# K and V of eight heads on 128 partitions: 8 KB rows, V under four quarter masks, one KV product of 260 columns

## Chip, cores, metric

One core of one Trainium2 chip. The metric is device time in microseconds (us). "Span" is the time from the first to the last instruction of a profiled execution. Ratios are the mean time of one kernel's fast runs over that of the other's fast runs of the same rounds, so they are not quite the ratio of the medians quoted beside them.

## The reference

Linear attention with ReLU features, batch 8, 12 heads, sequence 512, head size 64, all fp32:

```python
Q_feat = np.maximum(0, Q); K_feat = np.maximum(0, K)
KV    = np.einsum('bhkd,bhkv->bhdv', K_feat, V)
K_sum = np.sum(K_feat, axis=2)
numerator   = np.einsum('bhqd,bhdv->bhqv', Q_feat, KV)
denominator = np.einsum('bhqd,bhd->bhq', Q_feat, K_sum)
return (numerator / (denominator[:, :, :, None] + 1e-10)).astype(np.float32)
```

Each of Q, K, V and the output is 12.58 MB. The arithmetic is small; the traffic is not.

## The kernel before

It works in 12 octets (eight heads). Q is loaded by octets (a partition holds 32 rows of 64, 8 KB in DRAM), K and V by half octets (16 rows, 4 KB). All loads but the first are cast to bf16 on the way, from GpSimd's queue. To multiply several heads at once, K is written twice under a mask (even and odd heads) and V twice (left and right half of the partitions), with a column of ones that gives the sum of K. The product of a half octet accumulates over 16 rows into 130 columns.

```python
    def load_kv(g):                                   # a half octet
        k_sb[g] = kin.tile([P, R, D], bf16, name="k_sb")
        nc.gpsimd.dma_start(out=k_sb[g].rearrange("p r d -> p (r d)"), in_=Kr[g])
        v_sb[g] = vin.tile([P, R, D], bf16, name="v_sb")
        nc.gpsimd.dma_start(out=v_sb[g].rearrange("p r d -> p (r d)"), in_=Vr[g])
    ...
    def prep(g):
        for s in range(2):
            nc.vector.tensor_scalar(kf[g][:, :, s, :], k_sb[g], scalar1=0.0,
                                    scalar2=mask[:, 0, s:s + 1], op0=Alu.max, op1=Alu.mult)
        nc.vector.tensor_scalar(vo[g % NB][:, :, 0, 0:D], v_sb[g], scalar1=mask[:, 1, 0:1], ...)
    def prep_act(g):
        nc.scalar.activation(vo[g % NB][:, :, 1, 0:D], v_sb[g], Act.Copy, scale=mask[:, 1, 1:2])
    def mm_kv(g):
        ps_kv[g] = pkv.tile([P, 2, D1], fp32, name="ps_kv")
        for r in range(R):
            nc.tensor.matmul(ps_kv[g], kf[g][:, r, :, :]..., vo[g % NB][:, r, :, :], ...)
    def evac_kv(g):                                   # 4 copies, PSUM to SBUF, on ACT
        ...
    def store(o, o_sb):
        if o + DELAY < NO:                            # waits until K of octet o + 5 is there
            nc.sync.dma_start(out=scratch, in_=k_sb[2 * (o + DELAY)][0:1, 0, :])
        ...
    for o in range(NO + 1):
        mm_kv(2 * o); evac_kv(2 * o)
        mm_out(o - 1, 0); norm(o - 1, 0, o_sb)
        prep(2 * o + 2); prep_act(2 * o + 2)
        mm_out(o - 1, 1); norm(o - 1, 1, o_sb)
        mm_kv(2 * o + 1); evac_kv(2 * o + 1)
        for i in range(2):
            transp(o, i); evac_qt(o, i)
        prep(2 * o + 3); prep_act(2 * o + 3)
        mm_out(o - 1, 2); norm(o - 1, 2, o_sb); store(o - 1, o_sb)
```

(The conditions for the first and last rounds of the loop are cut, and some arguments, marked by dots.) The order in this loop is the order on each engine. The stores are held back on purpose: until the loads end, each waits for K five octets ahead, so that some five octets of output are still to be stored when the last load lands.

Of the kernel before, what the change touches and what calls it, by code (L numbers as in the profile page):

```python
# [10 lines left out]
def kernel(  # L11
# [7 lines left out]
    nc = tc.nc  # L19
    B, H, S, D = Q.shape  # L20
    assert D == 64
    P = 128
    D1 = D + 1
    NH = B * H


    R = S * 4 // P
    RQ = S * 8 // P
    NHG = 4
    U = RQ // 2  # L30
    NG = NH // NHG
    NO = NG // 2
    assert NO * 8 == NH and R == 16 and RQ == 32
    DELAY = 5
    F32 = 2

    fp32 = mybir.dt.float32
    bf16 = mybir.dt.bfloat16
    Act = mybir.ActivationFunctionType
    Alu = mybir.AluOpType  # L40

    def pool(name, bufs, **kw):
        return ctx.enter_context(tc.tile_pool(name=name, bufs=bufs, **kw))

    consts = pool("consts", 1)
    qin = pool("qin", 7)
    kin = pool("kin", 12)
    vin = pool("vin", 12)
    kfp = pool("kfp", 4)
    rcp = pool("rcp", 4)  # L50
    outp = pool("outp", DELAY + 2)
    pkv = pool("pkv", 2, space=bass.MemoryType.PSUM)
# [3 lines left out]
    def view(X, f):  # L56
        return X.rearrange("b h s d -> (b h s d)").rearrange("(n p f) -> n p f", p=P, f=f)

    Qr, Kr, Vr, Or = view(Q, RQ * D), view(K, R * D), view(V, R * D), view(out, RQ * D)

    ident = consts.tile([P, P], bf16, name="ident")
    NB = 4
    NK = 4
    NZ = 2




    vo = [consts.tile([P, R, 2, D1], bf16, name=f"vo{i}") for i in range(NB)]
    kvf = [consts.tile([P, NHG * 2 * D1], bf16, name=f"kvd{i}") for i in range(NK)]  # L70
    kvd = [x.rearrange("p (t s c d) -> p t s c d", t=2, s=2, c=2) for x in kvf]
    mask = consts.tile([P, 2, 2], fp32, name="mask")
    scratch = consts.tile([1, D], bf16, name="scratch")


# [4 lines left out]

    q_sb, k_sb, v_sb = {}, {}, {}

    def load_kv(g):
        k_sb[g] = kin.tile([P, R, D], bf16, name="k_sb")
        nc.gpsimd.dma_start(out=k_sb[g].rearrange("p r d -> p (r d)"), in_=Kr[g])  # L85
        v_sb[g] = vin.tile([P, R, D], bf16, name="v_sb")
        nc.gpsimd.dma_start(out=v_sb[g].rearrange("p r d -> p (r d)"), in_=Vr[g])  # L87

    def load_q(o):
        q_sb[o] = qin.tile([P, U, 2 * D], bf16, name="q_sb")  # L90
        nc.gpsimd.dma_start(out=q_sb[o].rearrange("p u f -> p (u f)"), in_=Qr[o])  # L91


    for g in range(F32):
        kv = outp.tile([P, 2, R, D], fp32, name="kv_first", tag="o_sb")
        k_sb[g], v_sb[g] = kv[:, 0], kv[:, 1]
        nc.sync.dma_start(out=k_sb[g].rearrange("p r d -> p (r d)"), in_=Kr[g])
        nc.scalar.dma_start(out=v_sb[g].rearrange("p r d -> p (r d)"), in_=Vr[g])
    load_q(0)
    make_identity(nc, ident)  # L100
    for o in range(1, NO):
        load_kv(2 * o)
        load_kv(2 * o + 1)
        load_q(o)

    def zero(i):
        if i == 0:
            for h in range(NHG):
                for s in range(2):
                    nc.vector.memset(mask[32 * h:32 * h + 32, 0, s:s + 1], 1.0 if h % 2 == s else 0.0)  # L110
            for t in range(2):
                nc.vector.memset(mask[:, 1, t:t + 1], 0.0)
                nc.vector.memset(mask[64 * t:64 * t + 64, 1, t:t + 1], 1.0)
        if i < NB:
            nc.vector.memset(vo[i][:, :, :, D:D1], 0.0)
            for t in range(2):
                nc.vector.memset(vo[i][64 * t:64 * t + 64, :, t, D:D1], 1.0)
        nc.vector.memset(kvf[i].bitcast(fp32), 0.0)  # L118

    def zero_q(i):  # L120
        nc.vector.memset(qtf[i].rearrange("p z f -> p (z f)").bitcast(fp32), 0.0)  # L121

    kf, ps_kv, ps_qt, ps_out = {}, {}, {}, {}

    def prep(g):
        kf[g] = kfp.tile([P, R, 2, D], bf16, name="kf")
        for s in range(2):
            nc.vector.tensor_scalar(kf[g][:, :, s, :], k_sb[g], scalar1=0.0,  # L128
                                    scalar2=mask[:, 0, s:s + 1], op0=Alu.max, op1=Alu.mult)
        nc.vector.tensor_scalar(vo[g % NB][:, :, 0, 0:D], v_sb[g], scalar1=mask[:, 1, 0:1],  # L130
                                scalar2=None, op0=Alu.mult)

    def prep_act(g):
        nc.scalar.activation(vo[g % NB][:, :, 1, 0:D], v_sb[g], Act.Copy, scale=mask[:, 1, 1:2])  # L134

    def mm_kv(g):
        ps_kv[g] = pkv.tile([P, 2, D1], fp32, name="ps_kv")
        for r in range(R):
            nc.tensor.matmul(  # L139
                ps_kv[g], kf[g][:, r, :, :].rearrange("p s d -> p (s d)"), vo[g % NB][:, r, :, :],  # L140
                start=(r == 0), stop=(r == R - 1), skip_group_check=True)

    def evac_kv(g):
        for s in range(2):
            for c in range(2):
                nc.scalar.copy(kvd[g % NK][64 * c:64 * c + 64, :, s, c, :],  # L146
                               ps_kv[g][64 * s:64 * s + 64])


    def transp(o, i):  # L150
        ps_qt[o, i] = pqt.tile([P, U // 2, P], bf16, name="ps_qt")
        for u in range(U // 2):
            nc.tensor.transpose(ps_qt[o, i][:, u, :], q_sb[o][:, i * (U // 2) + u, :], ident)  # L153
# [10 lines left out]
    def mm_out(o, j):  # L164
        po = pou.tile([P, 2, 512], fp32, name="ps_out")
        ps_out[o, j] = po
        u0, nu = ROUNDS[j]
        for v in range(nu):
            u, b, c = u0 + v, v // (nu // 2), v % (nu // 2) * 2 * D1
            for z in range(2):  # L170
                for w in range(4):
                    hs = slice(32 * w, 32 * w + 32)
                    h = 2 * w + z
                    nc.tensor.matmul(  # L174
                        po[hs, b, c:c + 2 * D1],
                        qtf[o % NZ][:, z, u * P + 32 * w:u * P + 32 * w + 32],
                        kvd[(2 * o + h // 4) % NK][:, h % 4 // 2, h % 2, :, :],
                        start=(z == 0), stop=(z == 1), skip_group_check=True)

    def norm(o, j, o_sb):  # L180
        u0, nu = ROUNDS[j]
        pv = ps_out[o, j][:, :, 0:nu * D1].rearrange("p b (r d) -> p b r d", d=D1)
        den = rcp.tile([P, 2, nu], fp32, name="den")
        nc.vector.tensor_scalar(den, pv[:, :, :, D], scalar1=1e-10, scalar2=None, op0=Alu.add)  # L184
        rec = rcp.tile([P, 2, nu], fp32, name="rec")
        nc.vector.reciprocal(rec, den)  # L186
        nc.vector.tensor_tensor(  # L187
            o_sb[:, 2 * u0:2 * (u0 + nu)].rearrange("p (b r) d -> p b r d", b=2),
            pv[:, :, :, 0:D],
            rec.unsqueeze(3).to_broadcast([P, 2, nu, D]), op=Alu.mult)  # L190
# [3 lines left out]

    def store(o, o_sb):
        if o + DELAY < NO:
            nc.sync.dma_start(out=scratch, in_=k_sb[2 * (o + DELAY)][0:1, 0, :])
        parts = 2 if o == NO - 1 else 1
        n = RQ // parts
        for j in range(parts):  # L200
            rs = slice(n * j, n * (j + 1))
            nc.sync.dma_start(out=Or[o].rearrange("p (r d) -> p r d", d=D)[:, rs], in_=o_sb[:, rs])

    zero(0)
    prep(0)
    prep_act(0)
    zero(1)
    prep(1)
    prep_act(1)
    zero_q(0)  # L210
    for k in range(2, NK):
        zero(k)
    zero_q(1)

    for o in range(NO + 1):
        ahead = o + 1 < NO
        if o > 0:
            o_sb = outp.tile([P, RQ, D], fp32, name="o_sb", tag="o_sb")
        if o < NO:
            mm_kv(2 * o)  # L220
            evac_kv(2 * o)
        if o > 0:
            mm_out(o - 1, 0)
            norm(o - 1, 0, o_sb)
        if ahead:
            prep(2 * o + 2)
            prep_act(2 * o + 2)
        if o > 0:
            mm_out(o - 1, 1)
            norm(o - 1, 1, o_sb)  # L230
        if o < NO:
            mm_kv(2 * o + 1)
            evac_kv(2 * o + 1)
            for i in range(2):
                transp(o, i)
                evac_qt(o, i)
        if ahead:
            prep(2 * o + 3)
            prep_act(2 * o + 3)
        if o > 0:  # L240
            mm_out(o - 1, 2)
            norm(o - 1, 2, o_sb)
            store(o - 1, o_sb)
# [28 lines left out]
```

## Time and profile before

| | kernel before |
|---|---|
| time, median of 4 runs | 128.07 us |
| span of the profiled run | 126.2 us |
| HBM read, written | 37.75 MB, 12.58 MB |
| mean granted TensorE clock | 0.905 |
| last Q load, last data packet ended | 111.2 us |
| last output ready, last store landed | 120.0, 125.1 us |

The first four rows are from the results and the page. The last two come from the records of single DMA packets and from the timeline. Read with the DMA slices in the prediction below: the sixteen DMA engines work from start to end; what compute must do is to be ready with the last octets while older stores still go out.

### The profile page before, as it was taken

The page shows a single profiled execution, that of the slowest core. Times are in us where ns is not written, and L with a number is a line of the kernel's source. Part 1 is how long each engine was busy: PE and PEld are TensorE (multiplying, and loading weights), DVE is VectorE, ACT ScalarE, POOL GpSimd, SP SyncE. Part 2 cuts the span into 40 slices and gives each one's busy share as a digit, 9 for nine tenths or more (in the row PEclk, how much of TensorE's full clock was granted, in tenths as well). Part 3 has the DMA queues.
Part 4 walks back from the last instruction along what each step waited for, and adds up shares of the span by engine and source line. Part 5 has one row for each costly group of instructions (what it writes and reads, how often), then busy time and mean ns, then how long its engine had stood idle before and what let it go on. Part 6 is the DMA issues. An engine that isn't in the chain of part 4 may idle for free.

```text
span 126.2 us, 4865 instructions
## 1 busy us (share of the span) xinstructions
PE 77.3 (61%) x2112; PEld 68.3 (54%) x2112; DVE 80.6 (64%) x210; ACT 76.9 (61%) x169; POOL 32.1 (25%) x62
## 2 busy tenths in 40 slices
PE   0032917978397956534997647389964793797200
PEld 0041907967386845434986646178953692696100
DVE  3256785698936959673669787528828628774900
ACT  0165891599198798660799949508917925958000
POOL 6902424325243331241143133033113000000000
PEclk9999999999859999996799999955999679769995
DMA  3999999999999999999999999999999999999992
GB/s 106 374 309 213 214 208 209 217 206 218 205 215 209 208 214 324 257 216 325 256 215 301 280 214 281 301 212 214 347 235 216 316 266 216 352 418 410 416 384 104
DMA packets 10757, 32.81 MB, mean 260 GB/s; under 512 B 1392, under 2 KB 1392, under 8 KB 9328
## 3 DMA queue, kind: packets, MB, share of 16 engines
q0 software_dynamic: 8064, 17.83, 73.9%
q1 hardware_dynamic: 2384, 13.63, 27.1%
q10 hardware_dynamic: 288, 1.05, 2.1%
q8 instruction: 16, 0.26, 0.7%
q14 instruction: 5, 0.04, 0.1%
HBM read 37.75 MB, written 12.58 MB: 399 GB/s over the span
## 4 chain that ended last, share of the span: by engine, by line
DMA 32%; PE 27%; issue 13%; ACT 11%; DVE 10%; ACTq 1%; SPq 0%
DMA v_sb<-in_V_dram 25%; PE ps_out L174 13%; PE ps_kv L139 11%; DMA kv_first<-in_K_dram 7%; ACT kvd L146 5%; ACT qt L159 4%; PE ps_qt L153 3%; DVE o_sb L187 3%; DVE qt L121 3%; ACT vo L134 3%; DVE kf L128 2%; DVE vo L130 1%; DVE rec L186 1%; ACTq L267 0%; DVE kvd L118 0%
## 5 line engine op out<-in xcount | busy, mean ns | idle before, releaser
L139 PE MATMUL ps_kv<-vo,kf 128*128 128x130 bf16 x384 | 32.5, 248 | 21.9 <-ACT vo L134 11.7
L174 PE MATMUL ps_out<-kvd,qt 128*32 128x130 bf16 x1536 | 33.7, 243 | 16.7 <-issue 13.3
L139 PEld LDWEIGHTS <-kf 128*128 128x128 bf16 x384 | 27.8, 112 | 25.3 <-DVE vo L130 16.3
L174 PEld LDWEIGHTS <-qt 128*32 128x32 bf16 x1536 | 27.0, 107 | 21.9 <-issue 15.3
L146 ACT CAST kvd<-ps_kv 64x130 bf16<-64x130 f32 x96 | 25.2, 263 | 16.7 <-PE ps_kv L139 14.8
L134 ACT ACTIVATE vo<-v_sb,mask 128x1024 bf16<-128x1024 bf16 x22 | 26.2, 1190 | 13.9 <-DMA v_sb<-in_V_dram 13.8
L187 DVE TENSOR_TENSOR o_sb<-ps_out,rec 128x768 f32<-128x768 f32 (+1 forms) x36 | 31.3, 868 | 1.4
L159 ACT ACTIVATE qt<-ps_qt 128x512 bf16<-128x512 bf16 x48 | 24.8, 603 | 0.3
L128 DVE TENSOR_SCALAR kf<-k_sb,mask 128x1024 bf16<-128x1024 bf16 x44 | 19.1, 476 | 8.6 <-DMA k_sb<-in_K_dram 8.6
L85 POOL DMA_DIRECT2D k_sb<-in_K_dram x22 | 12.8, 583 | 39.1 <-DMA q_sb<-in_Q_dram 24.1
L184 DVE TENSOR_SCALAR den<-ps_out 128x12 f32<-128x12 f32 (+1 forms) x36 | 5.9, 164 | 17.9 <-PE ps_out L174 17.8
L153 PE MATMUL ps_qt<-ident,q_sb 128*128 128x128 bf16 x192 | 15.7, 245 | 2.4 <-issue 2.4
L87 POOL DMA_DIRECT2D v_sb<-in_V_dram x22 | 12.3, 557 | 17.1 <-DMA k_sb<-in_K_dram 7.3
L153 PEld LDWEIGHTS <-q_sb 128*128 128x128 bf16 x192 | 14.0, 112 | 2.6 <-issue 2.5
L130 DVE TENSOR_SCALAR vo<-v_sb,mask 128x1024 bf16<-128x1024 bf16 x22 | 10.6, 481 | 2.1 <-DMA v_sb<-in_V_dram 2.1
L186 DVE RECIPROCAL rec<-den 128x12 f32<-128x12 f32 (+1 forms) x36 | 7.9, 220 | 1.2
L91 POOL DMA_DIRECT2D q_sb<-in_Q_dram x12 | 6.5, 542 | 7.8 <-DMA v_sb<-in_V_dram 4.1
L128 DVE TENSOR_SCALAR kf<-kv_first,mask 128x1024 bf16<-128x1024 f32 x4 | 2.8, 750 | 4.9 <-DMA kv_first<-in_K_dram 4.9
L134 ACT ACT_TABLE_LOAD x1 | 1.3, 1283 | 5.8 <-DMA kv_first<-in_V_dram 5.8
L121 DVE MEMSET qt<- 128x2048 f32 x2 | 3.5, 1765 | 0.8 <-issue 0.8
L134 ACT ACTIVATE vo<-kv_first,mask 128x1024 bf16<-128x1024 f32 x2 | 2.4, 1180 | 2.6 <-DMA kv_first<-in_V_dram 2.6
L130 DVE TENSOR_SCALAR vo<-kv_first,mask 128x1024 bf16<-128x1024 f32 x2 | 1.5, 747 | 0.0
(12 smaller groups left out, 3.5 us busy)
## 6 DMA issues: line engine op xcount, KB each, us to landing
out_dram<-o_sb SPq DMA_DIRECT2D x11, 1024.0 KB, 9.2
q_sb<-in_Q_dram POOLq DMA_DIRECT2D x12, 512.0 KB, 14.9
k_sb<-in_K_dram POOLq DMA_DIRECT2D x22, 256.0 KB, 13.8
v_sb<-in_V_dram POOLq DMA_DIRECT2D x22, 256.0 KB, 13.2
kv_first<-in_V_dram ACTq DMA_DIRECT2D x2, 512.0 KB, 7.3
kv_first<-in_K_dram SPq DMA_DIRECT2D x2, 512.0 KB, 7.0
out_dram<-o_sb SPq DMA_DIRECT2D x2, 512.0 KB, 5.1
scratch<-k_sb SPq DMA_DIRECT2D x7, 0.1 KB, 5.1
```

Of the source, the lines that this page charges most:

```text
L85: nc.gpsimd.dma_start(out=k_sb[g].rearrange("p r d -> p (r d)"), in_=Kr[g])
L87: nc.gpsimd.dma_start(out=v_sb[g].rearrange("p r d -> p (r d)"), in_=Vr[g])
L128: nc.vector.tensor_scalar(kf[g][:, :, s, :], k_sb[g], scalar1=0.0, scalar2=mask[:, 0, s:s + 1], op0=Alu.max, op1=Alu.mult)
L130: nc.vector.tensor_scalar(vo[g % NB][:, :, 0, 0:D], v_sb[g], scalar1=mask[:, 1, 0:1], scalar2=None, op0=Alu.mult)
L134: nc.scalar.activation(vo[g % NB][:, :, 1, 0:D], v_sb[g], Act.Copy, scale=mask[:, 1, 1:2])
L139: nc.tensor.matmul(ps_kv[g], kf[g][:, r, :, :].rearrange("p s d -> p (s d)"), vo[g % NB][:, r, :, :], start=(r == 0), stop=(r == R - 1), s ...
L146: nc.scalar.copy(kvd[g % NK][64 * c:64 * c + 64, :, s, c, :], ps_kv[g][64 * s:64 * s + 64])
L153: nc.tensor.transpose(ps_qt[o, i][:, u, :], q_sb[o][:, i * (U // 2) + u, :], ident)
L159: nc.scalar.activation(qtz[o % NZ][:, z, us, :, z, :], pv[:, :, :, z, :], Act.Relu)
L174: nc.tensor.matmul(po[hs, b, c:c + 2 * D1], qtf[o % NZ][:, z, u * P + 32 * w:u * P + 32 * w + 32], kvd[(2 * o + h // 4) % NK][:, h % 4 // ...
L186: nc.vector.reciprocal(rec, den)
L187: nc.vector.tensor_tensor(o_sb[:, 2 * u0:2 * (u0 + nu)].rearrange("p (b r) d -> p b r d", b=2), pv[:, :, :, 0:D], rec.unsqueeze(3).to_broa ...
```

## The change

Intent: K and V get the 8 KB rows that Q already has (half as many transfers, fewer packets), and the KV product of an octet becomes one accumulation with 260 columns, so that half as many evacuations are needed. The price: a partition now holds one of eight heads, so V must be written four times, each under the mask of a quarter of the partitions. There are fewer buffers too: three half octets of masked K and of V where there were four. Core of the diff:

```diff
-    def load_kv(g):
-        k_sb[g] = kin.tile([P, R, D], bf16, name="k_sb")
-        nc.gpsimd.dma_start(out=k_sb[g]..., in_=Kr[g])
+    def load_kv(o):
+        k_sb[o] = kin.tile([P, RQ, D], bf16, name="k_sb")
+        nc.gpsimd.dma_start(out=k_sb[o]..., in_=Kr[o])
 ... (V alike; the first octet, fp32:)
+    for i in range(2):
+        rs = slice(i * R, (i + 1) * R)
+        nc.sync.dma_start(out=k_sb[0][:, rs], in_=Kr[0].rearrange("p (r d) -> p r d", d=D)[:, rs])
+        nc.scalar.dma_start(out=v_sb[0][:, rs], in_=Vr[0].rearrange("p (r d) -> p r d", d=D)[:, rs])
+    nc.gpsimd.memset(mask_h, 1.0)                     # and two affine_selects on it
     load_q(0)
 ...
-        nc.vector.tensor_scalar(vo[g % NB][:, :, 0, 0:D], v_sb[g], scalar1=mask[:, 1, 0:1], ...)
+        for t in range(NT - 1 - g % 2):               # 3 of 4 quarters, or 2
+            nc.vector.tensor_scalar(vo[g % NB][:, :, t, 0:D], half(v_sb, g),
+                                    scalar1=mask_t[:, t:t + 1], scalar2=None, op0=Alu.mult)
     def prep_act(g):
-        nc.scalar.activation(vo[g % NB][:, :, 1, 0:D], v_sb[g], Act.Copy, scale=mask[:, 1, 1:2])
+        for t in range(NT - 1 - g % 2, NT):           # 1 of 4, or 2
+            nc.scalar.activation(vo[g % NB][:, :, t, 0:D], half(v_sb, g), Act.Copy,
+                                 scale=mask_t[:, t:t + 1])
     def mm_kv(g):
-        ps_kv[g] = pkv.tile([P, 2, D1], fp32, name="ps_kv")
+        if i == 0:
+            ps_kv[o] = pkv.tile([P, NT, D1], fp32, name="ps_kv")
 ... (one evac_kv for an octet, after mm_kv(2 * o + 1))
```

`half(x, g)` is the first or second 16 rows of an octet's tile. Both halves of an octet now come with one transfer of K and one of V.

More of the change, by code (lines that the diff above doesn't have):

```diff
@@ L24 @@
     NH = B * H
-    R = S * 4 // P
     RQ = S * 8 // P
-    NHG = 4
+    R = RQ // 2
     U = RQ // 2
-    NG = NH // NHG
-    NO = NG // 2
-    assert NO * 8 == NH and R == 16 and RQ == 32
+    NT = 4
+    NO = NH // 8
+    assert NO * 8 == NH and RQ == 32
     DELAY = 5
-    F32 = 2
     fp32 = mybir.dt.float32
@@ L46 @@
     qin = pool("qin", 7)
-    kin = pool("kin", 12)
-    vin = pool("vin", 12)
-    kfp = pool("kfp", 4)
+    kin = pool("kin", 6)
+    vin = pool("vin", 6)
+    kfp = pool("kfp", 3)
     rcp = pool("rcp", 4)
@@ L57, in view @@
         return X.rearrange("b h s d -> (b h s d)").rearrange("(n p f) -> n p f", p=P, f=f)
-    Qr, Kr, Vr, Or = view(Q, RQ * D), view(K, R * D), view(V, R * D), view(out, RQ * D)
+    Qr, Kr, Vr, Or = view(Q, RQ * D), view(K, RQ * D), view(V, RQ * D), view(out, RQ * D)
     ident = consts.tile([P, P], bf16, name="ident")
-    NB = 4
-    NK = 4
+    NB = 3
+    NK = 3
     NZ = 2
-    vo = [consts.tile([P, R, 2, D1], bf16, name=f"vo{i}") for i in range(NB)]
-    kvf = [consts.tile([P, NHG * 2 * D1], bf16, name=f"kvd{i}") for i in range(NK)]
-    kvd = [x.rearrange("p (t s c d) -> p t s c d", t=2, s=2, c=2) for x in kvf]
-    mask = consts.tile([P, 2, 2], fp32, name="mask")
+    vo = [consts.tile([P, R, NT, D1], bf16, name=f"vo{i}") for i in range(NB)]
+    kvf = [consts.tile([P, NT * 4 * D1], bf16, name=f"kvd{i}") for i in range(NK)]
+    kvd = [x.rearrange("p (t s c d) -> p t s c d", t=NT, s=2, c=2) for x in kvf]
+    mask_s = consts.tile([P, 2], fp32, name="mask_s")
+    mask_h = consts.tile([P, 2, NT], fp32, name="mask_h")
+    mask_t = consts.tile([P, NT], fp32, name="mask_t")
     scratch = consts.tile([1, D], bf16, name="scratch")
@@ L81 @@
     q_sb, k_sb, v_sb = {}, {}, {}
-    def load_kv(g):
-        k_sb[g] = kin.tile([P, R, D], bf16, name="k_sb")
-        nc.gpsimd.dma_start(out=k_sb[g].rearrange("p r d -> p (r d)"), in_=Kr[g])
-        v_sb[g] = vin.tile([P, R, D], bf16, name="v_sb")
-        nc.gpsimd.dma_start(out=v_sb[g].rearrange("p r d -> p (r d)"), in_=Vr[g])
+    def load_kv(o):
+        k_sb[o] = kin.tile([P, RQ, D], bf16, name="k_sb")
+        nc.gpsimd.dma_start(out=k_sb[o].rearrange("p r d -> p (r d)"), in_=Kr[o])
+        v_sb[o] = vin.tile([P, RQ, D], bf16, name="v_sb")
+        nc.gpsimd.dma_start(out=v_sb[o].rearrange("p r d -> p (r d)"), in_=Vr[o])
     def load_q(o):
@@ L91, in load_q @@
         nc.gpsimd.dma_start(out=q_sb[o].rearrange("p u f -> p (u f)"), in_=Qr[o])
-    for g in range(F32):
-        kv = outp.tile([P, 2, R, D], fp32, name="kv_first", tag="o_sb")
-        k_sb[g], v_sb[g] = kv[:, 0], kv[:, 1]
-        nc.sync.dma_start(out=k_sb[g].rearrange("p r d -> p (r d)"), in_=Kr[g])
-        nc.scalar.dma_start(out=v_sb[g].rearrange("p r d -> p (r d)"), in_=Vr[g])
+    k_sb[0] = outp.tile([P, RQ, D], fp32, name="k_first", tag="o_sb")
+    v_sb[0] = outp.tile([P, RQ, D], fp32, name="v_first", tag="o_sb")
+    for i in range(2):
[3 more added lines that the diff above has]
+    nc.gpsimd.memset(mask_h, 1.0)
+    for base, mult, lo in ((0, 1, -16), (15, -1, 16)):
+        nc.gpsimd.affine_select(
+            out=mask_h, in_=mask_h, pattern=[[lo, 2], [2 * lo, NT]], compare_op=Alu.is_ge,
+            fill=0.0, base=base, channel_multiplier=mult)
     load_q(0)
@@ L101 @@
     for o in range(1, NO):
-        load_kv(2 * o)
-        load_kv(2 * o + 1)
+        load_kv(o)
         load_q(o)
@@ L107, in zero, with zero_kv @@
         if i == 0:
-            for h in range(NHG):
-                for s in range(2):
-                    nc.vector.memset(mask[32 * h:32 * h + 32, 0, s:s + 1], 1.0 if h % 2 == s else 0.0)
-            for t in range(2):
-                nc.vector.memset(mask[:, 1, t:t + 1], 0.0)
-                nc.vector.memset(mask[64 * t:64 * t + 64, 1, t:t + 1], 1.0)
-        if i < NB:
-            nc.vector.memset(vo[i][:, :, :, D:D1], 0.0)
-            for t in range(2):
-                nc.vector.memset(vo[i][64 * t:64 * t + 64, :, t, D:D1], 1.0)
+            nc.vector.memset(mask_t, 0.0)
+            for t in range(NT):
+                nc.vector.memset(mask_t[32 * t:32 * t + 32, t:t + 1], 1.0)
+            nc.vector.tensor_reduce(out=mask_s, in_=mask_h, op=Alu.add, axis=mybir.AxisListType.X)
+        nc.vector.memset(vo[i][:, :, :, D:D1], 0.0)
+        for t in range(NT):
+            nc.vector.memset(vo[i][32 * t:32 * t + 32, :, t, D:D1], 1.0)
+    def zero_kv(i):
         nc.vector.memset(kvf[i].bitcast(fp32), 0.0)
@@ L123, with half @@
     kf, ps_kv, ps_qt, ps_out = {}, {}, {}, {}
+    def half(x, g):
+        return x[g // 2][:, g % 2 * R:g % 2 * R + R]
     def prep(g):
@@ L127, in prep, with evac_kv @@
         for s in range(2):
-            nc.vector.tensor_scalar(kf[g][:, :, s, :], k_sb[g], scalar1=0.0,
-                                    scalar2=mask[:, 0, s:s + 1], op0=Alu.max, op1=Alu.mult)
-        nc.vector.tensor_scalar(vo[g % NB][:, :, 0, 0:D], v_sb[g], scalar1=mask[:, 1, 0:1],
-                                scalar2=None, op0=Alu.mult)
+            nc.vector.tensor_scalar(kf[g][:, :, s, :], half(k_sb, g), scalar1=0.0,
+                                    scalar2=mask_s[:, s:s + 1], op0=Alu.max, op1=Alu.mult)
+        for t in range(NT - 1 - g % 2):
+            nc.vector.tensor_scalar(vo[g % NB][:, :, t, 0:D], half(v_sb, g),
+                                    scalar1=mask_t[:, t:t + 1], scalar2=None, op0=Alu.mult)
     def prep_act(g):
-        nc.scalar.activation(vo[g % NB][:, :, 1, 0:D], v_sb[g], Act.Copy, scale=mask[:, 1, 1:2])
+        for t in range(NT - 1 - g % 2, NT):
+            nc.scalar.activation(vo[g % NB][:, :, t, 0:D], half(v_sb, g), Act.Copy,
+                                 scale=mask_t[:, t:t + 1])
     def mm_kv(g):
-        ps_kv[g] = pkv.tile([P, 2, D1], fp32, name="ps_kv")
+        o, i = g // 2, g % 2
+        if i == 0:
+            ps_kv[o] = pkv.tile([P, NT, D1], fp32, name="ps_kv")
         for r in range(R):
             nc.tensor.matmul(
-                ps_kv[g], kf[g][:, r, :, :].rearrange("p s d -> p (s d)"), vo[g % NB][:, r, :, :],
-                start=(r == 0), stop=(r == R - 1), skip_group_check=True)
-    def evac_kv(g):
+                ps_kv[o], kf[g][:, r, :, :].rearrange("p s d -> p (s d)"), vo[g % NB][:, r, :, :],
+                start=(i == 0 and r == 0), stop=(i == 1 and r == R - 1), skip_group_check=True)
+    def evac_kv(o):
         for s in range(2):
             for c in range(2):
-                nc.scalar.copy(kvd[g % NK][64 * c:64 * c + 64, :, s, c, :],
-                               ps_kv[g][64 * s:64 * s + 64])
+                nc.scalar.copy(kvd[o % NK][64 * c:64 * c + 64, :, s, c, :],
+                               ps_kv[o][64 * s:64 * s + 64])
     def transp(o, i):
@@ L172, in mm_out @@
                     hs = slice(32 * w, 32 * w + 32)
-                    h = 2 * w + z
                     nc.tensor.matmul(
@@ L176, in mm_out @@
                         qtf[o % NZ][:, z, u * P + 32 * w:u * P + 32 * w + 32],
-                        kvd[(2 * o + h // 4) % NK][:, h % 4 // 2, h % 2, :, :],
+                        kvd[o % NK][:, w, z, :, :],
                         start=(z == 0), stop=(z == 1), skip_group_check=True)
@@ L196, in store @@
         if o + DELAY < NO:
-            nc.sync.dma_start(out=scratch, in_=k_sb[2 * (o + DELAY)][0:1, 0, :])
+            nc.sync.dma_start(out=scratch, in_=k_sb[o + DELAY][0:1, 0, :])
         parts = 2 if o == NO - 1 else 1
@@ L209 @@
     prep_act(1)
+    zero_kv(0)
     zero_q(0)
-    for k in range(2, NK):
-        zero(k)
+    zero(2)
+    zero_kv(1)
+    zero_kv(2)
     zero_q(1)
@@ L220 @@
             mm_kv(2 * o)
-            evac_kv(2 * o)
         if o > 0:
@@ L232 @@
             mm_kv(2 * o + 1)
-            evac_kv(2 * o + 1)
+            evac_kv(o)
             for i in range(2):
```

## The prediction

> **What bounds the kernel now.** I read the page's busy shares, the slices, the chain, the groups, then the timeline of the last 20 us and the records of single DMA packets. The engines first:
>
> ```profile
> PE 77.3 (61%) x2112; PEld 68.3 (54%) x2112; DVE 80.6 (64%) x210; ACT 76.9 (61%) x169; POOL 32.1 (25%) x62
> ...
> DMA  3999999999999999999999999999999999999992
> GB/s 106 374 309 213 214 208 209 217 206 218 205 215 209 208 214 324 257 216 325 256 215 301 280 214 281 301 212 214 347 235 216 316 266 216 352 418 410 416 384 104
> ...
> q0 software_dynamic: 8064, 17.83, 73.9%
> ...
> DMA 32%; PE 27%; issue 13%; ACT 11%; DVE 10%; ACTq 1%; SPq 0%
> ```
>
> No compute engine is over 64%, while DMA is at 9 in 38 of 40 slices. The rate counts what lands: casting loads land half of what they read, so 209 to 217 is 418 to 434 GB/s of reading, and the stores alone at the end make 410 to 418. The transfers (37.75 MB read, 12.58 written) fill the span, and the change moves the same bytes. Yet 10% of the chain is DVE, 11% ACT, 27% PE: compute follows closely, and at the end it must hand over the last outputs before the stores run out.
>
> The operations that the change touches:
>
> ```profile
> L139 PE MATMUL ps_kv<-vo,kf 128*128 128x130 bf16 x384 | 32.5, 248 | 21.9 <-ACT vo L134 11.7
> L146 ACT CAST kvd<-ps_kv 64x130 bf16<-64x130 f32 x96 | 25.2, 263 | 16.7 <-PE ps_kv L139 14.8
> L134 ACT ACTIVATE vo<-v_sb,mask 128x1024 bf16<-128x1024 bf16 x22 | 26.2, 1190 | 13.9 <-DMA v_sb<-in_V_dram 13.8
> L130 DVE TENSOR_SCALAR vo<-v_sb,mask 128x1024 bf16<-128x1024 bf16 x22 | 10.6, 481 | 2.1 <-DMA v_sb<-in_V_dram 2.1
> ```
>
> And the tail, from the timeline, after V of the next-to-last half octet becomes visible at 105.3:
>
> ```profile
> 105.38 1.18 ACT L134 ACTIVATE vo<-v_sb,mask 128x1024 bf16<-128x1024 bf16 x1 [3.54 <-DMA v_sb<-in_V_dram]
> ...
> 106.58 1.13 ACT L146 CAST kvd<-ps_kv 64x130 bf16<-64x130 f32 x4
> ...
> 107.73 2.06 ACT L159 ACTIVATE qt<-ps_qt 128x512 bf16<-128x512 bf16 x4
> ...
> 109.66 1.21 ACT L134 ACTIVATE vo<-v_sb,mask 128x1024 bf16<-128x1024 bf16 x1
> ...
> 110.72 1.12 ACT L146 CAST kvd<-ps_kv 64x130 bf16<-64x130 f32 x4
> 111.32 1.65 PE L139 MATMUL ps_kv<-vo,kf 128*128 128x130 bf16 x16
> ...
> 113.06 1.13 ACT L146 CAST kvd<-ps_kv 64x130 bf16<-64x130 f32 x4 [1.22 <-PE ps_kv L139]
> ...
> 114.21 2.06 ACT L159 ACTIVATE qt<-ps_qt 128x512 bf16<-128x512 bf16 x4
> ...
> 119.33 0.69 DVE L187 TENSOR_TENSOR o_sb<-ps_out,rec 128x512 f32<-128x512 f32 x1
> ```
>
> ACT is nearly the whole path from 105.4 to 114.2; the last output is ready at 120.0, 14.6 us after that V. The last store lands 5.1 us later, at 125.1, behind others that still queue. Its own 0.5 MB needs some 4.2 us (1.5 from issue to first packet, 1.25 at 420 GB/s, 1.4 from last packet to the waiting engine, all read off this trace), so compute has only about 1 us of slack at the end.
>
> **What the Trainium skill says.** "DMA: Bandwidth & Descriptors", section "Where 436 GB/s comes from", puts the ceiling at 435 GB/s; the trace agrees with its 418 to 434: longer rows have little left to win. "ScalarE: Activation LUTs", section "What ACT_TABLE_LOAD costs", gives 0.833 ns for each element of a row, plus 186 ns and 93 ns for a scale by pointer: 1132 for 1024 elements, where this trace has 1190, so the slope is usable. "TensorE: Matmul & The Clock Gate", section "Back-to-back issue gap", gives N/2.4 + 2.5 ns warm, 57 for 130 columns; the trace has 16 in 1.04 us, 65 each. Its section "The HAM clock gate" says that an idle array drops to half clock; the trace's lowest slices grant 0.5 to 0.6, mostly after a gap of PE.
>
> **The change part by part.**
>
> Loads. By the packet records, when only loads run, a K or V transfer of 4 KB rows follows the one before by 1.253 us (0.524 MB, 418 GB/s), and a Q transfer of 8 KB rows by 2.46 us (1.05 MB, 426 GB/s). So 22 pairs of K or V save 2.506 - 2.46 = 0.046 us each: 1.0 us. If only that counted: 128.06 - 1.0 = 127.0. The two extra mask steps on POOL before the first Q load cost some 0.8 us there, but 2.1 MB of first K and V keep the DMA busy.
>
> V under quarter masks, 4 x 24 writes in place of 2 x 24: DVE 60 instead of 24 (36 x 0.48 = +17 us, 98 in all, 78%), ACT 36 instead of 24 (12 x 1.19 = +14). Evacuation: 48 of 260 columns instead of 96 of 130. Estimate for one: 263 + 130 x 0.833 = 371 ns; 17.8 against 25.2 us, -7.4. ACT in sum 84 us. KV products: 384 as before but 260 columns, by the page 111 ns in a row against 65 measured now: +46 x 384 = +18 us of PE's streaming.
>
> None of these sums reaches the span. What counts is the loop through ACT and PE that an octet cannot shorten: second half's products after its V is written (16 x 0.111 + 0.3 = 2.1), evacuation at a pitch of 0.39 (1.6), the transposed Q (2.06), the next two quarter writes (2.4): 8.1 us for an octet. DVE needs 4 x 0.43 + 5 x 0.40 + 1.34 + 1.34 + 1.11 = 7.5 by the pitches in the timeline. Before, the same loop has 1.3 + 1.13 + 2.06 + 1.19 plus the first half's write and evacuation (2.3), about 8.0 where all chain up, but half of it can overlap; it really went at 7.8 an octet while behind its loads (K writes at 18.4 for the first, 73.1 for the eighth). PE also stands still with no visible cause:
>
> ```profile
> PE ps_out L174 <- issue: 13.3, 8, 3.6
> ```
>
> These gaps stay (as many PE instructions), about 1.7 us an octet with the other lines' issue time, and PE has only 1.3 of slack in the new loop. I put the new pace at 8.9, between 8.1 and 9.7. Loads come every 7.4 us at first, and 10 once stores share the DMA from about 45 us on. The first octet's last quarter write should end near 23 us (DVE's start is longer: five fp32 V writes of 0.75 instead of two), the last octet's thus at 23 + 10 x 8.9 = 112, if data never lacks.
>
> Tail. V of the last octet is now one load and both its halves wait for all of it. It takes the place of the last half octet's V, whose last packet ended at 107.35, visible about 108.7, less the 1.0 gained: 107.7, not 105.3. From there on ACT: quarter write 1.2, evacuation 1.6, Q 2.06, two writes 2.4 (7.3, at 115.0); then products 2.1, evacuation 1.6, first half of Q and output products 2.0, three normalizations 3.8: 16.8 in all, ready at 124.5. That the 112 lies below 115 says the pace just keeps up. The last half store then has no queue ahead of it: +4.2 is 128.7, +1.1 to the end of the span as now (126.2 - 125.1), +1.86 between span and time (128.06 - 126.2): 131.7 us. I take 131.5.
>
> **The rivals.**
> (a) DMA stays the only bound: 127.0. For it: DMA at 9 throughout, idle time on engines below 80%. Against: 1 us of slack at the end is less than what the tail gains in length.
> (b) The pace falls behind: at 9.7 an octet the last quarter write ends at 120 instead of 115 and the time is 136.5. For it: chain of PE, ACT and DVE up to 73 us already before, PE's gaps, a half clock doubling 1.8 us of products. Against: from 45 us on a period of 10 lets it catch up 1.1 an octet.
> (c) Fewer instructions and fewer waits (48 evacuations less, 22 loads less to issue) make the tail shorter than worked out, and DMA and compute end together: 128.5 to 129.5, within 2%.
> (d) 8 KB rows help more than Q shows: at the ceiling of 435 all through, 2% at most; the stores and Q already have such rows and make 410 to 426, which speaks against it.
>
> **Range and chances.** Tail with 1 us of error in V's time, 1 in its length, and the pace's 3 to 5 to one side: 127.5 to 136.0. Under 125.5 nothing but (d) leads: 0.03. Within 2% (125.5 to 130.6): (a), (c) and the short side of the tail, 0.38. Slower by over 2%: 0.59.
>
> **What would show it.** Right: q0's share falls by about 1%; ACT's quarter writes 36 x 1.19, DVE's 60 x 0.48, evacuation near 0.37, 16 KV products in about 1.8 us; ACT's wait for the last V ends near 107.7; last output near 124.5, DMA's last slices below 9 as stores wait for outputs. Wrong: DMA at 9 until the end with the last output before 121 would be (a) or (c); ACT never waiting for V after 60 us would be (b); a DVE write of the odd quarter offsets slower than 0.48 would add to DVE's 7.5 and make it the bound.

## The result

131.74 us median (131.35 to 131.96, 4 runs) against 128.07 (128.06 to 128.16): ratio 1.0288, 95% interval 1.0265 to 1.0312. Slower; 131.5 had been predicted.

From the page of the changed kernel: engines, the DMA slices, and the groups that answer to those of before.

```profile
PE 90.6 (70%) x2112; PEld 73.8 (57%) x2112; DVE 95.4 (73%) x242; ACT 82.6 (64%) x133; POOL 20.3 (16%) x43
...
DMA  4899999999999999999999999999999999997762
GB/s 87 241 325 252 212 213 213 213 212 218 211 217 209 214 211 280 305 216 275 309 216 268 318 209 270 312 217 210 314 271 235 310 257 265 416 414 303 288 262 114
...
L152 PE MATMUL ps_kv<-vo,kf 128*128 128x260 bf16 x384 | 51.9, 291 | 22.5 <-DVE vo L139 17.0
...
L144 ACT ACTIVATE vo<-v_sb,mask_t 128x1024 bf16<-128x1024 bf16 x33 | 36.9, 1184 | 8.3 <-DMA v_sb<-in_V_dram 8.3
...
L159 ACT CAST kvd<-ps_kv 64x260 bf16<-64x260 f32 x48 | 18.0, 374 | 20.2 <-PE ps_kv L152 19.7
...
L139 DVE TENSOR_SCALAR vo<-v_sb,mask_t 128x1024 bf16<-128x1024 bf16 x55 | 23.7, 482 | 0.8 <-DMA v_sb<-in_V_dram 0.8
...
out_dram<-o_sb SPq DMA_DIRECT2D x2, 512.0 KB, 3.3
```

The operations cost what was worked out (374 ns for an evacuation, 482 for a quarter write on DVE). The DMA has holes in its last four slices (7, 7, 6, 2), where before only the last slice was low: stores wait for outputs. And the second slice holds 241 where before it held 374: the start is slower, which nobody had expected.

The tail, from the timeline of the changed kernel (start, duration, engine, line, operation, out<-in, count, and in brackets the idle time before and what ended it), beginning when ACT sees the last V:

```profile
108.87 1.19 ACT L144 ACTIVATE vo<-v_sb,mask_t 128x1024 bf16<-128x1024 bf16 x1 [2.85 <-DMA v_sb<-in_V_dram]
...
109.97 1.53 ACT L159 CAST kvd<-ps_kv 64x260 bf16<-64x260 f32 x4
...
111.53 2.07 ACT L172 ACTIVATE qt<-ps_qt 128x512 bf16<-128x512 bf16 x4
...
113.46 2.24 ACT L144 ACTIVATE vo<-v_sb,mask_t 128x1024 bf16<-128x1024 bf16 x2
...
115.75 1.95 PE L152 MATMUL ps_kv<-vo,kf 128*128 128x260 bf16 x16 [0.27 <-ACT vo L144]
...
117.73 1.53 ACT L159 CAST kvd<-ps_kv 64x260 bf16<-64x260 f32 x4 [2.04 <-PE ps_kv L152]
...
119.29 2.06 ACT L172 ACTIVATE qt<-ps_qt 128x512 bf16<-128x512 bf16 x4
...
124.41 0.69 DVE L199 TENSOR_TENSOR o_sb<-ps_out,rec 128x512 f32<-128x512 f32 x1
```

From the last octet's first V write on ACT to the last output: 108.87 to 125.10, 16.2 us, against 105.38 to 120.02, 14.6 us, before (where only the first half of that V had to be there). The 3.7 us of the result add up from the two timelines: V is seen 3.5 us later (108.87 - 105.38), the chain behind it is 1.6 longer, the last store is through 1.8 sooner (3.3 against 5.1, as nothing queues ahead of it), and 0.4 lie behind the last landing.

### The profile page after: what moved, and what is told of

Its sections match the earlier page's. It is cut to its first block, busy times and chain, and to the rows that moved or that the text cites. A ratio compares the mean times of both kernels' runs of the same rounds, so it can differ in the third digit from the quotient of the medians.

```text
span 129.9 us, 4779 instructions
## 1 busy us (share of the span) xinstructions
PE 90.6 (70%) x2112; PEld 73.8 (57%) x2112; DVE 95.4 (73%) x242; ACT 82.6 (64%) x133; POOL 20.3 (16%) x43
## 3 DMA queue, kind: packets, MB, share of 16 engines
q0 software_dynamic: 4896, 17.83, 68.4%
## 4 chain that ended last, share of the span: by engine, by line
DMA 30%; PE 24%; ACT 23%; DVE 11%; issue 8%; ACTq 0%; SPq 0%
DMA v_sb<-in_V_dram 21%; PE ps_kv L152 16%; ACT vo L144 9%; DMA k_first<-in_K_dram 8%; ACT qt L172 7%; PE ps_out L186 6%; ACT kvd L159 6%; DVE qt L126 3%; DVE o_sb L199 2%; DVE vo L139 2%; DVE kf L136 2%; PE ps_qt L166 1%; DVE kvd L123 1%; DVE rec L198 1%; ACTq L280 0%
## 5 line engine op out<-in xcount | busy, mean ns | idle before, releaser
L152 PE MATMUL ps_kv<-vo,kf 128*128 128x260 bf16 x384 | 51.9, 291 | 22.5 <-DVE vo L139 17.0
L152 PEld LDWEIGHTS <-kf 128*128 128x128 bf16 x384 | 37.7, 102 | 33.0 <-DVE vo L139 17.6
L144 ACT ACTIVATE vo<-v_sb,mask_t 128x1024 bf16<-128x1024 bf16 x33 | 36.9, 1184 | 8.3 <-DMA v_sb<-in_V_dram 8.3
L186 PE MATMUL ps_out<-kvd,qt 128*32 128x130 bf16 x1536 | 29.7, 225 | 9.9 <-issue 7.8
L159 ACT CAST kvd<-ps_kv 64x260 bf16<-64x260 f32 x48 | 18.0, 374 | 20.2 <-PE ps_kv L152 19.7
L139 DVE TENSOR_SCALAR vo<-v_sb,mask_t 128x1024 bf16<-128x1024 bf16 x55 | 23.7, 482 | 0.8 <-DMA v_sb<-in_V_dram 0.8
L136 DVE TENSOR_SCALAR kf<-k_sb,mask_s 128x1024 bf16<-128x1024 bf16 x44 | 19.1, 475 | 0.0
L87 POOL DMA_DIRECT2D v_sb<-in_V_dram x11 | 6.1, 552 | 23.1 <-DMA q_sb<-in_Q_dram 12.4
L85 POOL DMA_DIRECT2D k_sb<-in_K_dram x11 | 6.3, 573 | 15.9 <-DMA v_sb<-in_V_dram 6.4
L139 DVE TENSOR_SCALAR vo<-v_first,mask_t 128x1024 bf16<-128x1024 f32 x5 | 3.5, 746 | 0.0
## 6 DMA issues: line engine op xcount, KB each, us to landing
out_dram<-o_sb SPq DMA_DIRECT2D x11, 1024.0 KB, 10.2
```

Source lines behind the costliest of these rows:

```text
L136: nc.vector.tensor_scalar(kf[g][:, :, s, :], half(k_sb, g), scalar1=0.0, scalar2=mask_s[:, s:s + 1], op0=Alu.max, op1=Alu.mult)
L139: nc.vector.tensor_scalar(vo[g % NB][:, :, t, 0:D], half(v_sb, g), scalar1=mask_t[:, t:t + 1], scalar2=None, op0=Alu.mult)
L144: nc.scalar.activation(vo[g % NB][:, :, t, 0:D], half(v_sb, g), Act.Copy, scale=mask_t[:, t:t + 1])
L152: nc.tensor.matmul(ps_kv[o], kf[g][:, r, :, :].rearrange("p s d -> p (s d)"), vo[g % NB][:, r, :, :], start=(i == 0 and r == 0), stop=(i = ...
L159: nc.scalar.copy(kvd[o % NK][64 * c:64 * c + 64, :, s, c, :], ps_kv[o][64 * s:64 * s + 64])
L186: nc.tensor.matmul(po[hs, b, c:c + 2 * D1], qtf[o % NZ][:, z, u * P + 32 * w:u * P + 32 * w + 32], kvd[o % NK][:, w, z, :, :], start=(z == ...
```

## The experiments

Theories: **T**, the chain that starts when the whole last V is seen sets the time; **P**, the pace: compute is behind its loads since the start; **D**, the DMA alone; **S**, the slow start comes from the first octet's half-row transfers. Each run also has runs of the kernel before on the same chip; the medians of these were 127.87 (first four), 128.16 (second four) and 127.95 (last four).

### 1. first_rows: the first octet in whole rows

```diff
-    for i in range(2):
-        rs = slice(i * R, (i + 1) * R)
-        nc.sync.dma_start(out=k_sb[0][:, rs], in_=...[:, rs])      # V alike, on ACT's queue
+    nc.sync.dma_start(out=k_sb[0]..., in_=Kr[0])
+    nc.scalar.dma_start(out=v_sb[0]..., in_=Vr[0])
```

> The changed kernel with the first octet's K and V loaded as whole 8 KB rows, one transfer each, in place of two transfers of half rows (4 KB pieces at an 8 KB pitch). Theory S (the half-row pieces made the start slow: 3.35 MB in the first 12 us against 3.98 in the kernel before): the first 12 us move about 4.0 MB, the last V is seen by ACT near 107.3 in place of 108.8, last output ready near 123.6, time about 130.3, ratio to the kernel before 1.017. Rival (the start is slow because the Q load is issued behind the mask steps, or by chance): 131.7, ratio 1.029, and still about 3.4 MB in 12 us.

Measured: 132.88 us, ratio 1.0384 (1.0347 to 1.0421). Slower still, though the start is mended: neither of the two expected times. From its page, DMA slices:

```profile
DMA  3999999999999999999999999999999999880662
GB/s 80 401 303 210 214 217 210 214 213 217 210 215 213 213 217 320 238 244 315 235 233 320 243 235 324 238 212 291 291 212 313 271 274 413 374 366 17 274 262 110
```

and from its waits (engine, line, what it waited for, us in total, times, longest):

```profile
ACT vo L142 <- DMA v_sb<-in_V_dram: 1.3, 1, 1.3
```

The second slice is back at 401 and the last load packet ends at 109.3 in place of 110.9. But ACT waits for V once, for the second octet, and never again: because the first product now needs the whole of V, it starts at 13.0 instead of 10.9, and compute never catches up. The 17 near the end is a DMA with nothing to store. So S is right for the DMA, and T as I had put it, with V's arrival alone at the end, is not enough: P takes over at once. Loads that end 1.6 us earlier bought nothing; the time even rose by more than 1 us.

### 2. q0_first: the Q load ahead of the mask steps

```diff
+    load_q(0)
     nc.gpsimd.memset(mask_h, 1.0)
     ...                                   # two affine_selects
-    load_q(0)
```

> The changed kernel with the first Q load issued before the two mask steps on POOL. Theory S (half rows are slow): Q's issue moves by 0.6 us only, no change of the time, 131.5 to 131.8. Rival (the order on POOL made the start slow): first Q packet near 5.3 us as in the kernel before in place of 7.0, time near 130.3.

Measured: 131.98 us (median of all four runs; 131.81 of the three fast ones), ratio 1.0299 (1.0264 to 1.0334). The profiled run fell in the slow state; only its first 12 us are read here. Its first Q packet went out at 6.7 us (7.0 in the changed kernel, 5.3 before), and the first 12 us moved 3.34 MB. In first_rows, with the mask steps still ahead of the Q load, Q's first packet went out at 5.8. The order on POOL is not the cause.

### 3. split_last: the last octet's K and V in half rows

```diff
+        parts = 2 if o == NO - 1 else 1
+        n = RQ // parts
+        for i in range(parts):
+            rs = slice(i * n, (i + 1) * n)
+            for x, X in ((k_sb, Kr), (v_sb, Vr)):
+                nc.gpsimd.dma_start(out=x[o][:, rs], in_=...[:, rs])
```

> The changed kernel with K and V of the last octet alone loaded in half rows (K half, V half, K half, V half). Theory T (the time is set by the chain that starts when the last V is seen, 108.8, because both halves wait for the whole): the first half is seen near 106, last output ready near 122.2 in place of 125.1, time near 129.3 (ratio 1.010). Rival P (compute has fallen behind its loads and granularity costs nothing): 131.5 or more. Rival D (DMA alone): 131.7 plus some tenths.

Measured: 130.84 us, ratio 1.0254 (1.0199 to 1.0309, unclear at 2%). Better than the changed kernel by 0.9 us in the medians and 0.4 by the ratios (the intervals overlap, so that even this is not sure), not by 2.4. ACT took up the first half of the last V at 106.34 after a wait of only 0.16: V came as early as expected, but compute was behind. ACT's next step, the evacuation of the octet before, had to wait 1.59 us for PE's products and began at 109.11, 0.9 earlier than in the changed kernel (109.97); the last output was ready at 124.69, 0.4 earlier. Neither T nor P alone.

### 4. rows_only: the old compute on the new rows (wrong result)

```diff
-    def load_kv(g): ...                   # half octet, 4 KB rows
+    def load_kv(o):
+        for x, pool_, X, name in ((k_sb, kin, Ko, "k_sb"), (v_sb, vin, Vo, "v_sb")):
+            t = pool_.tile([P, RQ, D], bf16, name=name)
+            nc.gpsimd.dma_start(out=t.rearrange("p r d -> p (r d)"), in_=X[o])
+            x[2 * o], x[2 * o + 1] = t[:, 0:R], t[:, R:RQ]
```

> Wrong result on purpose: the compute of the kernel before (two masks, products of 130 columns) fed from K and V in 8 KB rows from the second octet on; the first octet as before. Takes the change's extra compute away and keeps its loads. Theory T (both the whole V and the longer chain cost): V of the last octet is seen near 107.6, chain of 14.6 us from there, ready near 122.2, time 128.0 to 129.4. If the extra compute alone was the cause: 127.1 (the 1.0 us of faster rows shows). If the whole-octet load alone was: 131 or more.

Measured: 128.34 us, ratio 1.0042 (0.9990 to 1.0095). The result is wrong, as the masks do not fit the rows; the work is that of the kernel before. Timeline, when the last octet's V is seen and when its last output is made:

```profile
107.20 1.18 ACT L134 ACTIVATE vo<-v_sb,mask 128x1024 bf16<-128x1024 bf16 x1 [3.79 <-DMA v_sb<-in_V_dram]
...
121.36 0.69 DVE L187 TENSOR_TENSOR o_sb<-ps_out,rec 128x512 f32<-128x512 f32 x1
```

The chain is 14.85 us long (14.6 before), and starts 1.8 later than in the kernel before because V comes whole; that the last store now meets no queue (2.8 us from issue to landing against 5.1) hides most of that. Against this run the changed kernel is 3.4 us slower: V seen 1.7 later (the slow start), the chain 1.4 longer (16.2 against 14.85), the rest 0.3. So 8 KB rows by themselves are a draw: what the faster transfers give (the last load packet ends at 109.6 in place of 111.2), the coarser arrival takes.

### 5 and 6. act_mid and act_tail: spare work on ACT, off and on the path

```diff
+            if o == 6:                    # act_mid;  act_tail: o == NO - 2
+                for _ in range(2):
+                    nc.scalar.activation(spare, half(v_sb, 2 * o + 2), Act.Copy, scale=mask_t[:, 0:1])
             prep_act(2 * o + 3)
```

> The changed kernel with two spare quarter writes on ACT (2.24 us) just ahead of its pair of quarter writes in the seventh octet, near 78 us. Theory T (the tail that starts when the last V is seen sets the time, and compute has by then caught up with its loads): the waits of ACT for V near 89, 99 and 109 us (1.2 + 0.6 + 2.9 us) swallow it: 131.7 to 132.0. Rival P (pace: compute is behind throughout): +2.2, 133.9.

> The same two spare writes ahead of the last pair of quarter writes, near 113 us. T and P: on the path to the last products, +2.2, 133.9. Rival D (the stores alone set the end): 131.7 to 132.2.

Measured: act_mid 132.33 us, ratio 1.0338 (1.0284 to 1.0392); act_tail 134.28 us (median of all four runs; 134.09 of the three fast ones), ratio 1.0459 (1.0416 to 1.0501). Against the changed kernel's 1.0288 that is +0.6 and +2.2 us (ratio differences times 128.16) for the same 2.2 us of ACT. At the end it counts in full, so D is out as the only limit. In the middle most of it is swallowed: the +0.6 is not clear of the noise, as the two intervals overlap.

### 7. pool_zero: an earlier start for compute

```diff
+        if o == 2:                        # in the load loop, on GpSimd
+            for x in (kvf[0], qtf[0]..., kvf[1], kvf[2], qtf[1]...):
+                nc.gpsimd.memset(x.bitcast(fp32), 0.0)
...
-    zero_kv(0); zero_q(0)
     zero(2)
-    zero_kv(1); zero_kv(2); zero_q(1)
```

> The changed kernel with the zero fills of the transposed Q and of the KV tiles moved from VectorE to GpSimd (about 5 us of VectorE's start), so that compute starts up to 5 us earlier and has no backlog. T: no more than 0.3 us gained, 131.4 to 131.8, the last V is still seen near 108.8. P: 129.5 or less.

Measured: 131.27 us, ratio 1.0245 (1.0230 to 1.0261). From its waits and its timeline:

```profile
ACT vo L148 <- DMA v_sb<-in_V_dram: 16.8, 7, 3.4
...
108.99 1.18 ACT L148 ACTIVATE vo<-v_sb,mask_t 128x1024 bf16<-128x1024 bf16 x1 [3.18 <-DMA v_sb<-in_V_dram]
```

Compute now waits for V in each of the last six octets (8.3 us of such waits in the changed kernel, 16.8 now), and the last V is seen when it was. The time moves by about 0.5 us. With the backlog gone, V's arrival is the limit that stays.

### 8. pool_split: both limits lifted

Edits 3 and 7 together.

> pool_zero and split_last together. Reading of the first four runs: two limits lie within 1 us of each other, the last V's arrival and the pace since the start, so that lifting one alone (split_last) gave 0.9 us of the 2.4 expected. With both lifted: first half of the last V seen near 106, 129.3 (ratio 1.010). If split_last fell short for another reason (half rows, Q, stores): 130.5 or more.

Measured: 129.26 us, ratio 1.0089 (1.0073 to 1.0105). As expected. Timeline:

```profile
106.35 1.18 ACT L153 ACTIVATE vo<-v_sb,mask_t 128x1024 bf16<-128x1024 bf16 x1 [1.07 <-DMA v_sb<-in_V_dram]
...
121.83 0.69 DVE L208 TENSOR_TENSOR o_sb<-ps_out,rec 128x512 f32<-128x512 f32 x1
```

Alone, the two edits gave some 0.4 and 0.6 us by their ratios; together 2.5. That is the mark of two limits that lie side by side.

### 9 and 10. rows_pool_split and parts_pool_split: the start on top

rows_pool_split adds edit 1. parts_pool_split instead cuts the first loads by partitions, with whole rows:

```diff
+    for x, X in ((k_sb, Kr), (v_sb, Vr)):
+        for eng, ps in ((nc.sync, slice(0, P // 2)), (nc.scalar, slice(P // 2, P))):
+            eng.dma_start(out=x[0]...[ps], in_=X[0][ps])
```

> pool_split with the first octet's K and V as whole 8 KB rows, as in first_rows. Theory S (half-row pieces slow the first 12 us by 1.5 us of DMA time, hidden in first_rows because compute started 2 us later and never caught up): with compute's backlog gone the loads end 1.5 us earlier and the time follows: 127.7, ratio 0.997. Rival (later start of compute still decides): 129.3.

> The same, but K first and then V, each in two transfers of 64 partitions with whole 8 KB rows (one from each issuing engine). S: whole rows are what matters, 4.0 MB in the first 12 us, 127.7 or a little less as K comes first. If 64 partitions fill only half of the DMA engines, or if it was the number of transfers and not the half rows: 3.4 MB and 129.3.

Measured: rows_pool_split 128.47 us, ratio 1.0041 (1.0017 to 1.0066); parts_pool_split 130.91 us, ratio 1.0229 (1.0208 to 1.0249). Whole rows in one transfer from each queue bring 0.6 us here, where in first_rows they cost more than one: the backlog that they cause has been taken away. It is less than the 1.5 expected, because compute falls behind again. ACT saw the first half of the last V at 104.99, 1.4 us earlier than in pool_split (106.35), but the products of the octet before began only 1.0 earlier (104.37 against 105.33), and so did the last output come (121.56 against 122.52); another 0.2 went to the last store (4.0 against 3.8 us to land). Whole rows alone are not what matters: in two pieces of 64 partitions they were slower than either expectation (ACT's first V write at 15.6 us against 9.1 in pool_split, the last load packet's end at 115.5 against 112.5). S holds for the transfers as they are in the change; which property of a piece makes it slow, I can't say.

### 11. all_four: rows_pool_split with the last octet's V on VectorE as well

```diff
+    def n_dve(g):
+        return NT if g >= 2 * NO - 2 else NT - 1 - g % 2
-        for t in range(NT - 1 - g % 2):
+        for t in range(n_dve(g)):         # ACT: range(n_dve(g), NT)
```

> rows_pool_split with all quarter writes of the last octet on VectorE (3 writes of ACT off the path, 3 more on VectorE). If the chain from the last V through ACT still sets the end: 1.5 us less than rows_pool_split, 126.3 to 126.8; if the stores do (DMA at 9 to the end, floor estimated at 127.0): 127.0 to 127.7, no more than 0.5 less.

Measured: 128.38 us, ratio 1.0040 (1.0013 to 1.0068): the same as rows_pool_split, and above both expected ranges. From its page and its timeline:

```profile
DMA  4999999999999999999999999999999999999973
GB/s 83 408 304 210 215 215 212 209 220 211 212 215 218 209 214 262 302 216 276 312 214 257 321 225 232 328 241 212 308 280 214 329 250 218 359 417 412 386 291 157
...
out_dram<-o_sb SPq DMA_DIRECT2D x2, 512.0 KB, 3.3
...
108.71 1.67 DVE L149 TENSOR_SCALAR vo<-v_sb,mask_t 128x1024 bf16<-128x1024 bf16 x4
...
111.47 0.88 PE L196 MATMUL ps_out<-kvd,qt 128*32 128x130 bf16 x48 [1.43 <-DVE o_sb L209]
112.29 1.96 PE L162 MATMUL ps_kv<-vo,kf 128*128 128x260 bf16 x16
...
121.36 0.69 DVE L209 TENSOR_TENSOR o_sb<-ps_out,rec 128x512 f32<-128x512 f32 x1
```

The DMA's holes are gone but for the last two slices, as they were in pool_split and rows_pool_split already. At first sight the DMA ends it, since three writes off ACT's tail gave nothing. The timeline says otherwise: the chain did not get shorter, the work only moved. VectorE's V writes now hold up its normalizations, and PE stands still for 1.43 us until one of them is done. The last 16 KV products began at 112.29, against 112.15 in rows_pool_split, and the last output was ready at 122.05, against 121.56. Its store then landed in 3.3 us, as in the changed kernel, where nothing queued ahead; in rows_pool_split it took 4.0. So this run does not show that the DMA is the limit, and why 128.4 is above the 127.0 that I had put as the floor stays open. The uneven end of the loads is nothing new: the last sixteen completion records of the load queue lie between 107.2 and 112.4 us here, and between 107.5 and 111.5 in the kernel before. None of these versions beats the kernel before.

### 12. halves_all: half rows everywhere

Edit 3 without the condition, for all octets from the second on.

> The changed kernel with K and V of every octet in half rows. If half rows at an 8 KB pitch are slow in themselves (as the first loads were, 200 to 290 GB/s): over 145 us. If they are slow only in the first transfers: pairs at 2.50 instead of 2.46 us, loads end 1 us later, but the last V's first half is seen 2 us earlier: 130.5 to 131.8.

Measured: 130.74 us, ratio 1.0238 (1.0197 to 1.0279, unclear at 2%). Between 12 and 50 us 420 GB/s were read or written, against 426 in the changed kernel: half rows at an 8 KB pitch are not slow in themselves. The slow start belongs to the first transfers, issued from the two other queues.

## Why the prediction was right, step by step

- **Costs of single operations.** Evacuation 374 ns (371 worked out), quarter writes 1184 and 482 (1190, 481), as many as counted. The 16 products take 1.95 us with the last one's latency, a little over the 1.8: 119 ns each in the chain, not 111.
- **Loads.** Right: K and V octets follow each other by 2.46 us in the packet records, and between 50 and 105 us 420.7 GB/s are read or written against 417.0. But the sentence that the first K and V "keep the DMA busy" failed: in the first 12 us 3.35 MB moved instead of 3.98, which is 1.5 us at 420 GB/s. The rows themselves gained more than the 1.0 worked out: in rows_only, with the start of the kernel before, the last load packet ended 1.6 us earlier, and V was seen at 107.2. The slow start ate all of it, so that V was seen at 108.9 and not 107.7. (The sign that q0's share would fall by about 1% was too small as well: 73.9% to 68.4%.) The cause was not the mask steps that I had named there (run 2) but the cut of the first transfers (runs 1, 9).
- **Tail.** Right in kind and nearly in size: 16.2 us against 16.8. The term "+4.2" for the last store was 3.3. These two, 1.5 us in all, make up for V's 1.2 and for 0.4 more behind the last landing; that 131.7 came out so closely is partly luck.
- **Pace.** 8.9 us an octet was predicted; ACT's pairs of writes from 22.25 to 85.46 us are seven octets at 9.0. Undisturbed octets take 7.75; the rest are the first (12.9, with the cold start) and the octets with PE's gaps (up to 10.2). From 88 us on ACT waits for V again, as expected. What I had not drawn from "112 lies below 115" is that two limits so close must both be lifted: runs 1, 3, 7 and 8 show it.
- **Rivals.** (a) and (d), DMA alone, fall with the holes at the end and with act_tail. (b), the pace, is half right: not the limit at the end, but less than 1 us behind it (the 0.4 to 0.9 us that split_last alone gained). (c) is right in that the tail and the last store were shorter than worked out (by 0.6 and 0.9 us), but not by enough for its 129.5.

## What to carry to other kernels

Where transfers already run near their ceiling, as here, longer rows won about a per cent (1.6 us of 128), so ask what it costs at both ends: data that arrives in larger pieces starts the last chain later, and extra work on engines that look half idle lengthens that chain one for one. Where removing a suspect gives much less than it should, look for a second limit just behind it and lift both at once before giving up either. The start is part of the path when compute never catches up: a first product that came 2 us later, at 13 us, was still felt at the end. And before a time is read as "this work did not matter", look in the timeline whether the chain got shorter at all: in run 11 the work only went to another engine of the same chain.

## What the Trainium skill lacked or had wrong

- "DMA: Bandwidth & Descriptors" gives rates by transfer size; it has nothing on first loads from the two hardware queues (those of SP and ACT) whose rows are cut: here 512 KB pieces of half rows moved at 200 to 290 GB/s for some 4 us, while whole rows moved at about 400. Its advice in "Rules for kernel authors" not to cut a transfer into partition halves is borne out. It gives no price; here it was 130.91 us against 128.47, with K before V as a second difference.
- "TensorE: Matmul & The Clock Gate", section "Back-to-back issue gap": the prediction took its 57 and 111 ns from the formula N/2.4 + 2.5 ns, which the section gives for a single matmul; it says itself that this under-counts at small N where weight loads go along, and gives about 81 ns for N = 128 in such a stream. Measured here, with a weight load for each product, were 65 ns at 130 columns (16 in 1.04 us), which lies between the two, and 119 at 260 (16 in 1.90 us by the chain), a little over the formula's 111.
- "ScalarE: Activation LUTs", section "What ACT_TABLE_LOAD costs": the constant is high for the copies out of PSUM here. Estimated from the page's figures, 130 columns without a pointer scale take 294 ns and 260 take 403; here 263 and 374, thus 0.85 ns an element and about 152 ns besides.
- "Runtime: NRT & Kernel Launch", section "Instruction fetch mechanics", says that the program comes in 16 KiB blocks and that crossing into the next is "mostly hidden". Here it may not be hidden: each of the nine gaps of PE with no releaser in the changed kernel ends 1.4 to 1.6 us after a 16 KB packet on the queue that the profile calls "instruction" has ended (62.8 and 64.3, 87.8 and 89.3, 101.4 and 102.8, 107.6 and 109.2 us among them). That they are waits for the program is inferred from these times; no run tested it. The longest here, from the timeline:

```profile
64.28 0.24 PE L186 MATMUL ps_out<-kvd,qt 128*32 128x130 bf16 x3 [2.70 <-issue]
```
